# First stage of a two-layer fp32 trunk: modulation weights in row tiles, six convolution chunks in flight, a written order on the engines, later constants on the SP queue

## The chip, the cores and the metric

The kernel runs on one core of a Trainium2 chip. The metric is the device time of one execution in microseconds (us). A core has five engines that run beside each other: TensorE (PE; its weight loads are listed apart as PEld), VectorE (DVE), ScalarE (ACT), GpSimd (POOL) and SyncE (SP). Each takes its instructions in a fixed order, and semaphores hold one back until what it reads has been written. Data come from memory (HBM) by DMA transfers, which an engine's queue issues and 16 DMA engines carry out.

## What is computed

Two layers over 256 latent and 256 context tokens with 1024 features, all in fp32. Each layer modulates its input by a vector worked out from the condition, multiplies it by one wide matrix, and feeds three branches (attention, a depthwise convolution of width 31, pooling), which gates mix; then comes a feed-forward part. The change concerns the beginning of the first layer:

```python
def ada_mod(cond, w, b, n):
    m = jax.nn.silu(cond) @ w[:, :n * D_MODEL] + b[:n * D_MODEL]
    return m.reshape(m.shape[:-1] + (n, D_MODEL))
def modulate(h, shift, scale):
    return h * (1.0 + scale) + shift
...
ml = ada_mod(c, w_ada[l], b_ada[l], N_MOD)[:, None]
mc = ada_mod(c_ctx, w_ada[l], b_ada[l], 2 if last else N_MOD)
hl = modulate(x, ml[..., 0, :], ml[..., 1, :])
hc = modulate(ctx, mc[0], mc[1])
zl = hl @ w_in[l] + b_in[l]
...
# the convolution branch takes 2048 columns of z
a, gt = jnp.split(u, 2, axis=-1)
h = depthwise_conv(a * jax.nn.sigmoid(gt), dw_w, dw_b)
```

So nothing of `w_in` can be multiplied before shift and scale are known, and these need 2048 columns of `w_ada`: 8 MB.

## The kernel before

**Layout.** Activations lie transposed: features on the 128 partitions (eight blocks k of 128), 512 columns of tokens (latent 256, context 256). Each fp32 product is made as three products of fp32r numbers, hi by hi, lo by hi and hi by lo (`mm3`, L326 to L332), where hi is a rounded copy that ACT makes (L228 for weights, L530 for the modulated input) and lo the remainder that DVE subtracts (L229, L339).

**Weights.** They are streamed tile by tile in a written list, `ORDER` (L101). `load_to` (L199 to L212) issues transfers on the SP queue a few places ahead (`LA` = 6) into six raw buffers of 512 KB (`NRAW`); `split_to` (L216 to L230) makes hi and lo in five buffer pairs (`NW`); `take` (L232) hands out the next tile. `x` in the list is a 256 KB tile of the input.

**First stage** (L499 to L546). The modulation is made in four quarters q; each gives shift and scale for two blocks k. `ad0(q, kk)` multiplies the condition (32 columns `sc`) with a 512 KB tile of `w_ada`, four tiles for a quarter, 16 products each (L507). `ad0_end(q)` closes a quarter: DVE copies the row out of PSUM (L514), PE transposes it (L516), DVE adds the bias (L521) and 1 (L525), ACT makes the hi part of the two modulated blocks (L530, four activations), DVE h and its lo part (L531, L339). A convolution chunk is a 512 KB tile of `w_in` with 128 of its columns for all eight k: 24 products (3 by 8) into one PSUM bank. Four such chunks, conv 0 to 3, are started in this stage, each quarter adding the six products of its two k to each of the four banks, with the `ad0` tiles of the next quarter between them.

**Then** chunks conv 4 to 15 run whole (24 products). Chunks come in pairs: ACT takes the sigmoid `sg` of one (L604, its table is loaded first), DVE makes `gl` (L606), and for each two pairs it runs the depthwise taps `H` (L574 first, then L582), which have low priority. Behind conv 15 come the `kv` tiles, the queries, the gates, the pooling. Some 512 KB tiles of `w_ada` (`ada`, L277, eight products) for later modulations lie between the chunks.

**Order.** The Tile framework lays out each engine's order from the program's order and priorities. The constants `ct`, `ID`, `vt[0]`, `ic`, `gr`, `rt`, `vt[1]`, `cb` and the bias rows `bq` are loaded from ACT's queue. `cb` is 1 MB, the condition spread over the partitions, on which ACT then works a Silu (L906).

## Time and profile before

| what | value |
|---|---|
| time, median of 3 runs | 1467.37 us (1467.19 to 1468.29) |
| the profiled execution's own time | 1468.65 us |
| its span, from the first to the last instruction | 1466.8 us |
| PE busy / DVE busy / ACT busy | 1398.2 / 1097.1 / 697.5 us |
| mean granted TensorE clock | 0.986 |
| memory read | 209.83 MB, 144 GB/s over the span |

A row of the timeline reads: start in us, duration in us, engine, line, operation, output<-inputs, tile, count of instructions joined in the row, and in brackets the idle time of the engine before it with what released it. A row of the windows reads: stretch and its length in us, then busy time and count of instructions of each engine in it, the granted TensorE clock (1.00 is full speed, 0.50 half), the mean busy share of the DMA engines and the GB/s that they moved. In the page, a row of digits has one for each fortieth of the span: the busy share in tenths.

### The profile page before, as it was taken

The page shows a single profiled execution, that of the slowest core. Times are in us where ns is not written, and L with a number is a line of the kernel's source. Part 1 is how long each engine was busy: PE and PEld are TensorE (multiplying, and loading weights), DVE is VectorE, ACT ScalarE, POOL GpSimd, SP SyncE. Part 2 cuts the span into 40 slices and gives each one's busy share as a digit, 9 for nine tenths or more (in the row PEclk, how much of TensorE's full clock was granted, in tenths as well). Part 3 has the DMA queues.
Part 4 walks back from the last instruction along what each step waited for, and adds up shares of the span by engine and source line. Part 5 has one row for each costly group of instructions (what it writes and reads, how often), then busy time and mean ns, then how long its engine had stood idle before and what let it go on. Part 6 is the DMA issues. An engine that isn't in the chain of part 4 may idle for free.

```text
span 1466.8 us, 21501 instructions
## 1 busy us (share of the span) xinstructions
PE 1398.2 (95%) x8308; PEld 1207.3 (82%) x8308; DVE 1097.1 (75%) x1998; ACT 697.5 (48%) x1159; POOL 60.2 (4%) x61
## 2 busy tenths in 40 slices
PE   5999999999999998999999999989889989899997
...
DMA  9733332223233411534442677444423345355550
GB/s 368 266 121 131 108 108 94 79 73 121 81 122 130 154 69 58 172 139 162 158 141 93 237 246 251 138 137 139 142 87 130 122 159 181 124 184 187 174 172 29
DMA packets 62246, 212.28 MB, mean 145 GB/s; under 512 B 7104, under 2 KB 8256, under 8 KB 62016
## 3 DMA queue, kind: packets, MB, share of 16 engines
...
q8 instruction: 65, 1.06, 0.3%
...
HBM read 209.83 MB, written 1.05 MB: 144 GB/s over the span
## 4 chain that ended last, share of the span: by engine, by line
PE 64%; issue 15%; DVE 11%; ACT 3%; POOL 1%; DMA 1%; POOLq 0%; DVEq 0%; ACTq 0%
PE mm L330 19%; PE mm L331 19%; PE mm L332 19%; DVE H L582 5%; DVE lo L229 3%; PE ax L362 2%; PE ax L792 1%; PE ax L395 1%; ACT nat L419 1%; PE ad L277 1%; ACT hi L228 1%; DMA rawt<-in_wst 1%; PE ax L434 1%; POOL rotb L663 0%; PE ax L330 0%
## 5 line engine op out<-in xcount | busy, mean ns | idle before, releaser
L228 ACT ACTIVATE hi<-raw 128x1024 fp32r<-128x1024 f32 (+2 forms) x296 | 305.1, 1035 | 495.0 <-PE mm L331 398.8
L229 DVE TENSOR_TENSOR lo<-raw,hi 128x1024 fp32r<-128x1024 f32 (+2 forms) x296 | 353.5, 1197 | 140.0 <-ACT hi L228 134.7
L331 PE MATMUL mm<-hl,hi 128*128 128x256 f32 (+1 forms) x1112 | 353.1, 319 | 2.5 <-DVE hl L471 2.4
L330 PE MATMUL mm<-hh,hi 128*128 128x256 f32 (+1 forms) x1112 | 348.3, 320 | 6.3 <-ACT sg L604 3.2
L332 PE MATMUL mm<-hh,lo 128*128 128x256 f32 (+1 forms) x1112 | 351.6, 318 | 1.9 <-DVE lo L229 1.9
L582 DVE SCALAR_TENSOR_TENSOR H<-gl,vt,H 128x502 f32<-128x502 f32 (+29 forms) x480 | 265.4, 606 | 0.1
L331 PEld LDWEIGHTS mm<-hl,hi 128*128 128x128 f32 x1112 | 214.7, 193 | 18.5 <-DVE hl L471 3.8
L330 PEld LDWEIGHTS mm<-hh,hi 128*128 128x128 f32 x1112 | 211.4, 193 | 22.3 <-ACT sg L604 3.6
L332 PEld LDWEIGHTS mm<-hh,lo 128*128 128x128 f32 x1112 | 214.5, 193 | 16.1 <-DVE lo L229 2.5
L330 PE MATMUL mm<-hi,hi 128*128 128x512 f32 x480 | 192.5, 403 | 0.9 <-ACT hi L530 0.6
L332 PE MATMUL mm<-hi,lo 128*128 128x512 f32 x384 | 151.5, 394 | 0.0
L331 PE MATMUL mm<-llo,hi 128*128 128x512 f32 x384 | 151.2, 394 | 0.0
L330 PE MATMUL mm<-ah,hi 128*128 128x256 f32 (+1 forms) x374 | 123.1, 329 | 0.0
L332 PE MATMUL mm<-ah,lo 128*128 128x256 f32 (+1 forms) x374 | 122.8, 328 | 0.0
L331 PE MATMUL mm<-al,hi 128*128 128x256 f32 (+1 forms) x374 | 122.3, 327 | 0.0
L299 DVE CUSTOM_DVE_ANT_0 prod<-rawt,cb,vt 128x1024 f32<-128x1024 f32 x80 | 102.5, 1281 | 17.5 <-DMA rawt<-in_wst 16.6
L330 PEld LDWEIGHTS mm<-hi,hi 128*128 128x128 f32 x480 | 91.4, 191 | 27.1 <-issue 5.7
L332 PEld LDWEIGHTS mm<-hi,lo 128*128 128x128 f32 x384 | 72.5, 189 | 15.8 <-issue 0.4
L331 PEld LDWEIGHTS mm<-llo,hi 128*128 128x128 f32 x384 | 72.7, 189 | 15.2 <-issue 0.4
L331 PEld LDWEIGHTS mm<-al,hi 128*128 128x128 f32 x374 | 71.0, 190 | 6.0
L330 PEld LDWEIGHTS mm<-ah,hi 128*128 128x128 f32 x374 | 71.0, 190 | 6.0
L332 PEld LDWEIGHTS mm<-ah,lo 128*128 128x128 f32 x374 | 71.0, 190 | 6.0
(178 smaller groups left out, 2017.7 us busy)
## 6 DMA issues: line engine op xcount, KB each, us to landing
raw<-in_wst SPq DMA_DIRECT2D x312, 512.0 KB, 3.5
rawt<-in_wst SPq DMA_DIRECT2D x56, 512.0 KB, 4.1
...
x<-in_xT SPq DMA_DIRECT2D x8, 256.0 KB, 7.1
raw<-in_wst SPq DMA_DIRECT2D x8, 256.0 KB, 2.6
x<-in_xT ACTq DMA_DIRECT2D x8, 256.0 KB, 2.7
bq<-in_brow ACTq DMA_DIRECT2D x6, 256.0 KB, 4.0
...
```

The source lines that it names most:

```text
L228: A.activation(hi[:, :w], r[:, :w], AF.Copy)
L229: V.tensor_tensor(lo[:, :w], r[:, :w], hi[:, :w].bitcast(F32), op=ALU.subtract)
L277: PE.matmul(ps[32 * j:32 * j + 32, :], sc[:, k, :], w[:, j * 256:(j + 1) * 256], start=(k == 0), stop=(k == KT - 1),)
L299: tc.keep_in_program_order(V.tensor_tensor_reduce(prod, w, cb[:, s], 1.0, col(l, "b_ada", m * 8 + c), ALU.mult, ALU.add, mods[l, m][:, c, ...
L330: PE.matmul(ps, lh, rh, start=(first and i == 0), stop=False)
L331: PE.matmul(ps, lh, rl, start=False, stop=False)
L332: PE.matmul(ps, ll, rh, start=False, stop=(last and i == n - 1))
L362: PE.matmul(ps, x[:, a:b], y[:, c:d], start=(i == 0), stop=(i == n - 1))
L395: PE.transpose(a[:, tt * 256 + c2 * P:tt * 256 + (c2 + 1) * P], pair[c2][:, o:o + P], ID)
L419: A.activation(n[:, half(tt)], n[:, half(tt)], AF.Identity, scale=rs[:, tt:tt + 1], bias=nm[:, tt:tt + 1],)
L434: PE.transpose(a[:, c2 * 256 + tt * P:c2 * 256 + (tt + 1) * P], self.nat[i, s][:, o:o + P], ID)
L582: V.scalar_tensor_tensor(h[:, :, a:b], g[:, :, a + d:b + d], col(l, "dw_w", k * 8 + j), h[:, :, a:b], op0=ALU.mult, op1=ALU.add,)
```

## The change

- **Order.** `pin` keeps the instructions of PE, ACT and DVE in the first stage in program order while `strict` is set; the stage is written out as a list of calls. `load` chains the transfers on the SP queue in program order.
- **Six chunks.** conv 4 and conv 5 also start in the first stage, in banks of the `aux` pool; conv 5's hi and lo parts lie in four small `w` tiles, split half by half (there are five buffer pairs for hi and lo).
- **Row tiles.** The first `w_ada` tiles are 32 of 256 KB, 128 rows each, in place of 16 of 512 KB; the host lays them out so. `take` looks 14 places ahead (`LA0`) in this stage.
- **List.** All eight tiles of the first quarter come ahead of any `x`; conv 0 to 5 lie between the tiles of quarters 1 and 2, and quarter 3 is last.
- **Identity products.** 16 products of the identity with itself, into a bank that nobody reads, stand on PE between the first transpose and the first chunk.
- **Constants.** `gr`, `rt`, `vt[1]`, `ic`, `cb` and all `bq` move from the ACT queue to the SP queue, in program order behind weights.

On SP, at the program's start, the order was this (`raw` are weight tiles, `x` input tiles):

```order
L212 DMA raw_95<-in_wst 128x1024
L212 DMA raw_97<-in_wst 128x1024
L205 DMA x_99<-in_xT 128x512
L205 DMA x_101<-in_xT 128x512
L212 DMA raw_103<-in_wst 128x1024
L212 DMA raw_105<-in_wst 128x1024
L212 DMA raw_107<-in_wst 128x1024
L212 DMA raw_113<-in_wst 128x1024
L212 DMA raw_115<-in_wst 128x1024
```

And now it is this, from the first quarter's last tiles on (`ad` are the 256 KB tiles of `w_ada`):

```order
L202 DMA ad_108<-in_wst 128x512
L202 DMA x_110<-in_xT 128x512
L202 DMA x_112<-in_xT 128x512
L202 DMA raw_114<-in_wst 128x1024
L202 DMA raw_116<-in_wst 128x1024
L202 DMA ad_118<-in_wst 128x512
L202 DMA ad_120<-in_wst 128x512
L202 DMA ad_122<-in_wst 128x512
L202 DMA ad_129<-in_wst 128x512
L202 DMA raw_135<-in_wst 128x1024
```

The first quarter's 2 MB no longer have the two `x` tiles between them, and conv 0 (`raw_107` before, `raw_114` now) and conv 1 (`raw_115`, `raw_116`) follow directly on `x`.

On ACT, the program's beginning was this; row by row it issues constants and then works:

```order
L178 DMA ct<-in_cT 128x16
L179 DMA ID<-in_ident 128x128
L181 DMA vt_80<-in_vec 128x524
L183 DMA ic<-in_icnt 128x64
L265 ACT_TABLE_LOAD
L265 ACTIVATE sc<-ct 128x8x2
L617 DMA gr<-in_grow 128x512
L627 DMA vt_81<-in_vec 128x524
L628 DMA cb<-in_crow 128x2048
L637 DMA bq_1059<-in_brow 128x512
L906 ACTIVATE cb<-cb 128x2048
L228 ACTIVATE hi_109<-raw_107 128x1024
```

And now:

```order
L186 DMA ct<-in_cT 128x16
L187 DMA ID<-in_ident 128x128
L189 DMA vt_80<-in_vec 128x524
L297 ACT_TABLE_LOAD
L297 ACTIVATE sc<-ct 128x8x2
L564 ACTIVATE hi_195<-x_110,mod_0_91,one_p 128x256 x2
L564 ACTIVATE hi_203<-x_112,mod_0_91,one_p 128x256 x2
L260 ACTIVATE hi_217<-raw_114 128x1024
L260 ACTIVATE hi_224<-raw_116 128x1024
```

Five transfers and the Silu of `cb` have gone from here. On SP they now stand between weight tiles for chunks behind the first stage (`rt` is the rotation table, `raw_556` and `raw_880` weight tiles):

```order
L202 DMA raw_556<-in_wst 128x1024
L202 DMA gr<-in_grow 128x512
L202 DMA rt_765<-in_rope 128x512
L202 DMA vt_81<-in_vec 128x524
L202 DMA ic<-in_icnt 128x64
L202 DMA cb<-in_crow 128x2048
L202 DMA raw_880<-in_wst 128x1024
```

Before, SP had only weight tiles there. The Silu of `cb` now comes behind the sigmoid of conv 9, with a table load ahead of it and one behind.

On PE, between the first and the second round of chunk products, this stood before (`ad_335` and `ad_415` are quarters 2 and 3 of the modulation, `ax` a transposed row, `mm_197`, `mm_247` conv 0 and conv 1 with the blocks of quarter 1):

```order
L516 MATMUL ax_308<-ID,adarow_306 128x128
L507 MATMUL ad_335<-raw_215,sc 32x128 x8
L507 MATMUL ad_335<-raw_217,sc 32x128 x8
L507 MATMUL ad_335<-raw_223,sc 32x128 x8
L507 MATMUL ad_335<-raw_225,sc 32x128 x8
L516 MATMUL ax_388<-ID,adarow_386 128x128
L507 MATMUL ad_415<-raw_227,sc 32x128 x8
L507 MATMUL ad_415<-raw_229,sc 32x128
L330 MATMUL mm_197<-hi_313,hi_109 128x512
L330 MATMUL mm_247<-hi_313,hi_117 128x512
```

And this stands there now (`ax_305` is quarter 1's transposed row, `mm_316` conv 3 with quarter 0, `ad_345` quarter 2, `mm_221` conv 0 with quarter 1):

```order
L548 MATMUL ax_305<-ID,adarow_303 128x128
L362 MATMUL mm_316<-hi_195,hi_312 128x512
L363 MATMUL mm_316<-xlo_197,hi_312 128x512
L364 MATMUL mm_316<-hi_195,lo_313 128x512
L362 MATMUL mm_316<-hi_203,hi_312 128x512
L363 MATMUL mm_316<-xlo_205,hi_312 128x512
L364 MATMUL mm_316<-hi_203,lo_313 128x512
L540 MATMUL ad_345<-ad_215,sc 32x128 x4
L540 MATMUL ad_345<-ad_222,sc 32x128 x4
L540 MATMUL ad_345<-ad_235,sc 32x128 x4
L540 MATMUL ad_345<-ad_242,sc 32x128 x4
L362 MATMUL mm_221<-hi_317,hi_217 128x512
```

Before, all of quarter 2 and the beginning of quarter 3 (and the transfers they wait for) stood ahead of the second round; now half of quarter 2 does, and a chunk's products stand behind the transpose.

On PE at the program's start there is now (`ax_178` is the bank of the identity products, `mm_221` conv 0):

```order
L548 MATMUL ax_173<-ID,adarow_171 128x128
L582 MATMUL ax_178<-ID 128x128 x16
L362 MATMUL mm_221<-hi_195,hi_217 128x512
L363 MATMUL mm_221<-xlo_197,hi_217 128x512
L364 MATMUL mm_221<-hi_195,lo_218 128x512
```

Nothing stood between this transpose and the next `ad0` tiles before. Behind the first stage the orders of the engines agree but for the constants above and a few exchanges of neighbours; on DVE five lo parts (conv 6 to 10) stand ahead of the first tap, where four did (conv 4 to 7).

The diff, without the definitions of constants and the change to the host's layout:

```diff
+    first = [[("ad0", 0, q, k) for k in range(KT)] for q in range(4)]
+    xs = [[("x", 0, 2 * q), ("x", 0, 2 * q + 1)] for q in range(4)]
     o = weight_order(0)
-    conv = [x for x in o if x[0] == "conv"][:4]
-    res = first[0] + [conv[0]] + first[1][:1] + [conv[1]] + first[1][1:4] + [conv[2]] + first[1][4:5] + [conv[3]] + first[1][5:]
-    return res + first[2] + first[3] + [x for x in o if x not in conv] + weight_order(1)
+    conv = [x for x in o if x[0] == "conv"][:NCP]
+    res = first[0] + xs[0] + conv[:2] + first[1][:4] + conv[2:3] + first[1][4:] + conv[3:4] + xs[1]
+    res += first[2][:4] + conv[4:5] + first[2][4:] + conv[5:6] + xs[2] + xs[3] + first[3]
+    return res + [x for x in o if x not in conv] + weight_order(1)
...
+    def pin(ins):
+        return tc.keep_in_program_order(ins) if strict else ins
...
+    def load(dst, src, behind=True):
+        i = SP.dma_start(dst, src).ins
+        if behind and loads:
+            tc.add_manual_dep(
+                i, loads[-1].name, mybir.DependencyInfo(mybir.DependencyClass.NoSync, mybir.DependencyReason.DATA),
+                reason="order of loads",
+            )
+        loads.append(i)
...
+            if it[0] == "ad0":
+                raw[it] = S(name="ad0")
+                load(raw[it], wst[o:o + P * w].rearrange("(p c) -> p c", p=P))
...
+            if strict and it == ("conv", 0, 2, 1):
+                split[it] = tuple(tuple(S(F32R, "w") for _ in range(2)) for _ in range(2))
+                for x, (hi, lo) in enumerate(zip(*split[it])):
+                    rx = r[:, x * 512:(x + 1) * 512]
+                    pin(A.activation(hi, rx, AF.Copy))
+                    pin(V.tensor_tensor(lo, rx, hi.bitcast(F32), op=ALU.subtract))
+                continue
...
-            load_to(i + LA)
-            split_to(ahead[i])
+            load_to(i + (LA0 if strict else LA))
+            split_to(i if strict else ahead[i])
...
-    for kk in range(4):
-        ad0(0, kk)
+    ad0(0, range(8))
     ad0_end(0)
-    for q in range(4):
-        for i in range(4):
-            it = ("conv", 0, i // 2, i % 2)
-            if q == 0:
-                convpre[it] = take(it), mmb()
-            mm_by_k([convpre[it]], hT, (2 * q, 2 * q + 1), NTOK)
-            if q < 3:
-                ad0(q + 1, i)
-        if q < 3:
-            ad0_end(q + 1)
+    warm = aux()
+    for _ in range(NWARM):
+        pin(PE.matmul(warm[:, :P], ID, ID, start=True, stop=True))
+    scaled(0)
+    conv_take(0, 1)
+    conv_mm(0, 0)
+    ad0(1, range(4))
+    conv_mm(0, 1)
+    conv_take(2)
+    conv_mm(0, 2)
+    ad0(1, range(4, 8))
+    ad0_end(1)
+    conv_take(3)
+    scaled(1)
+    conv_mm(0, 3)
+    ad0(2, range(4))
+    conv_mm(1, 0, 1, 2, 3)
+    conv_take(4)
+    conv_mm(0, 4)
+    ad0(2, range(4, 8))
+    conv_mm(1, 4)
+    ad0_end(2)
+    conv_take(5)
+    scaled(2)
+    conv_mm(0, 5)
+    conv_mm(1, 5)
+    conv_mm(2, 0, 1, 2, 3)
+    ad0(3, range(8))
+    conv_mm(2, 4)
+    ad0_end(3)
+    scaled(3)
+    conv_mm(2, 5)
+    conv_mm(3, *range(NCP))
+    strict.clear()
...
-                A.dma_start(gr, grow[l:l + 1, :].to_broadcast([P, 512]).rearrange("p (a d) -> p a d", a=4))
+                load(gr, grow[l:l + 1, :].to_broadcast([P, 512]).rearrange("p (a d) -> p a d", a=4))
...
-                    A.dma_start(cb, crow.to_broadcast([P, 2 * D]).rearrange("p (s d) -> p s d", s=2))
+                    load(vt[1], vec[1])
+                    load(ic, icnt.to_broadcast([P, 64]).rearrange("p (g e t) -> p g e t", g=4, e=2))
+                    load(cb, crow.to_broadcast([P, 2 * D]).rearrange("p (s d) -> p s d", s=2))
...
-            A.dma_start(bq, brow[l:l + 1, boff:boff + 512].to_broadcast([P, 512]))
+            load(bq, brow[l:l + 1, boff:boff + 512].to_broadcast([P, 512]))
```

In the diff, `scaled(q)` holds L530, L531 and L339 of `ad0_end` as it was, `conv_take` takes chunks and gives them banks, and `conv_mm(q, ...)` adds quarter q's products to the chunks named.

More of the change, by code (lines that the diff above doesn't have):

```diff
@@ L35 @@
 LA = 6
+LA0 = 14
+NCP = 6
+NWARM = 16
 LS = 3
@@ L101, in full_order @@
 def full_order():
-    first = [
-        [("ad0", 0, q, 0), ("ad0", 0, q, 1), ("x", 0, 2 * q), ("x", 0, 2 * q + 1), ("ad0", 0, q, 2), ("ad0", 0, q, 3)]
-        for q in range(4)
-    ]
+    first = [[("ad0", 0, q, k) for k in range(KT)] for q in range(4)]
+    xs = [[("x", 0, 2 * q), ("x", 0, 2 * q + 1)] for q in range(4)]
     o = weight_order(0)
-    conv = [x for x in o if x[0] == "conv"][:4]
-    res = first[0] + [conv[0]] + first[1][:1] + [conv[1]] + first[1][1:4] + [conv[2]] + first[1][4:5] + [conv[3]] + first[1][5:]
-    return res + first[2] + first[3] + [x for x in o if x not in conv] + weight_order(1)
+    conv = [x for x in o if x[0] == "conv"][:NCP]
+    res = first[0] + xs[0] + conv[:2] + first[1][:4] + conv[2:3] + first[1][4:] + conv[3:4] + xs[1]
+    res += first[2][:4] + conv[4:5] + first[2][4:] + conv[5:6] + xs[2] + xs[3] + first[3]
+    return res + [x for x in o if x not in conv] + weight_order(1)
 ORDER = full_order()
@@ L118, in width @@
         return 0
-    if it[0] == "plw":
+    if it[0] in ("plw", "ad0"):
         return 512
@@ L204, in load_to @@
                 xr.append(S(name="x"))
-                SP.dma_start(xr[-1], xT[it[2]])
+                load(xr[-1], xT[it[2]])
+                nxt["load"] += 1
+                continue
+            if it[0] == "ad0":
+                raw[it] = S(name="ad0")
+                load(raw[it], wst[o:o + P * w].rearrange("(p c) -> p c", p=P))
                 nxt["load"] += 1
@@ L211, in load_to @@
                 t = wp.tile([P, CH], F32, tag="raw", name=f"raw{nxt['load']}", bufs=NRAW)
[L212 removed]
+            load(t[:, :w], wst[o:o + P * w].rearrange("(p c) -> p c", p=P), bool(strict) or it[0] == "adt")
             raw[it] = t
@@ L329, in mm3 @@
         for i, ((lh, ll), (rh, rl)) in enumerate(pairs):
-            PE.matmul(ps, lh, rh, start=(first and i == 0), stop=False)
-            PE.matmul(ps, lh, rl, start=False, stop=False)
-            PE.matmul(ps, ll, rh, start=False, stop=(last and i == n - 1))
+            pin(PE.matmul(ps, lh, rh, start=(first and i == 0), stop=False))
+            pin(PE.matmul(ps, lh, rl, start=False, stop=False))
+            pin(PE.matmul(ps, ll, rh, start=False, stop=(last and i == n - 1)))
     def part(hl, a, b):
+        if isinstance(hl[0], tuple):
+            return tuple(x[a // 512][:, a % 512:a % 512 + b - a] for x in hl)
         return hl[0][:, a:b], hl[1][:, a:b]
@@ L497, in trunk, with ad0 @@
     ad0_ps = {}
-    def ad0(q, kk):
-        w = take(("ad0", 0, q, kk))
-        if kk == 0:
-            ad0_ps[q] = pad.tile([P, 256], F32, tag="ad", name=uid("ad"))
-        for k2 in range(2):
-            for j in range(4):
-                o = k2 * 512 + j * P
-                PE.matmul(
-                    ad0_ps[q][32 * j:32 * j + 32, :P], sc[:, 2 * kk + k2, :], w[:, o:o + P],
-                    start=(kk + k2 == 0), stop=(kk + k2 == 4),
-                )
+    def ad0(q, ks):
+        for k in ks:
+            w = take(("ad0", 0, q, k))
+            if k == 0:
+                ad0_ps[q] = pad.tile([P, 256], F32, tag="ad", name=uid("ad"))
+            for j in range(4):
+                pin(PE.matmul(
+                    ad0_ps[q][32 * j:32 * j + 32, :P], sc[:, k, :], w[:, j * P:(j + 1) * P], start=(k == 0), stop=(k == KT - 1),
+                ))
     def ad0_end(q):
         row = sm(256, "adarow", bufs=1)
-        V.tensor_copy(row[:, :P], ad0_ps[q][:, :P])
+        pin(V.tensor_copy(row[:, :P], ad0_ps[q][:, :P]))
         pt = aux()
-        PE.transpose(pt[:, :P], row[:, :P], ID)
+        pin(PE.transpose(pt[:, :P], row[:, :P], ID))
         hk = slice(2 * q, 2 * q + 2)
@@ L526, in ad0_end, with scaled @@
+    def scaled(q):
         for k in (2 * q, 2 * q + 1):
-            hi, h32 = S(F32R, name="hi"), S(name="h32")
+            hi, h32, lo = S(F32R, name="hi"), S(name="h32"), S(F32R, name="xlo")
             for s in range(2):
                 sh, sl = mods[0, 0][:, k, s:s + 1], one_p[:, k, s:s + 1]
-                A.activation(hi[:, half(s)], xr[k][:, half(s)], AF.Identity, scale=sl, bias=sh)
-                V.tensor_scalar(h32[:, half(s)], xr[k][:, half(s)], sl, sh, op0=ALU.mult, op1=ALU.add)
```

33 lines of the change are left out of this document (21 added, 12 removed).

## The prediction

> **What bounds the kernel now.** First the page: the whole span, then its digits.
>
> ```profile
> span 1466.8 us, 21501 instructions
> PE 1398.2 (95%) x8308; PEld 1207.3 (82%) x8308; DVE 1097.1 (75%) x1998; ACT 697.5 (48%) x1159; POOL 60.2 (4%) x61
> PE   5999999999999998999999999989889989899997
> DMA  9733332223233411534442677444423345355550
> ```
>
> PE is busy 95% of the span, so the time follows what PE does; its one weak digit is the first (5), where the DMA engines show 9. So I cut the beginning into stretches with the windows.
>
> ```profile
> 0.00:12.00 12.00, 1.93 (x32) 1.38 (x32) 1.06 (x12) 1.50 (x2) 0.45 (x8) 1.00 0.79 290
> 12.00:22.00 10.00, 4.25 (x58) 2.50 (x59) 2.96 (x7) 4.74 (x5) 0.00 (x0) 1.00 1.03 409
> 22.00:36.00 14.00, 12.13 (x133) 7.54 (x128) 5.94 (x12) 5.37 (x9) 0.00 (x0) 0.98 1.03 405
> 36.00:44.00 8.00, 7.61 (x39) 5.43 (x36) 6.00 (x16) 2.07 (x4) 0.00 (x0) 0.60 1.03 404
> 44.00:62.40 18.40, 17.40 (x128) 11.85 (x126) 7.01 (x13) 6.79 (x9) 0.00 (x0) 1.00 0.63 229
> 66.00:123.00 57.00, 57.00 (x258) 46.61 (x257) 57.00 (x78) 13.51 (x15) 4.52 (x4) 1.00 0.36 126
> 123.00:143.00 20.00, 20.00 (x101) 15.41 (x100) 5.38 (x6) 5.03 (x6) 0.00 (x0) 1.00 0.40 137
> 182.00:187.00 5.00, 2.43 (x9) 2.04 (x10) 4.99 (x12) 3.45 (x18) 3.27 (x4) 0.88 0.19 44
> ```
>
> Up to 22 us PE works 6.2 us of 22, up to 44 the DMA engines are full at some 405 GB/s, and in 36 to 44 the granted clock is 0.60. From 66 to 123 PE and DVE are both full; in 123 to 143 DVE is free for 14.6 of 20 us; in 182 to 187 PE waits beside a full DVE. The timeline of PE shows what the first stage waits for.
>
> ```profile
> 12.81 1.08 PE L507 MATMUL ad<-raw,sc 128*32 128x128 f32 x16 [4.63 <-DMA raw<-in_wst]
> 15.91 1.08 PE L507 MATMUL ad<-raw,sc 128*32 128x128 f32 x16 [2.02 <-DMA raw<-in_wst]
> ...
> 22.46 1.22 PE L330 MATMUL mm<-hi,hi 128*128 128x512 f32 x2
> ...
> 24.79 0.63 PE L332 MATMUL mm<-hi,lo 128*128 128x512 f32 x1
> ...
> 31.46 0.27 PE L516 MATMUL ax<-ID,adarow 128*128 128x128 f32 x1
> 31.66 1.08 PE L507 MATMUL ad<-raw,sc 128*32 128x128 f32 x32
> 33.96 0.65 PE L507 MATMUL ad<-raw,sc 128*32 128x128 f32 x16 [1.22 <-DMA raw<-in_wst]
> ...
> 38.38 1.65 PE L330 MATMUL mm<-hi,hi 128*128 128x512 f32 x3
> ...
> 42.63 0.40 PE L332 MATMUL mm<-hi,lo 128*128 128x512 f32 x1
> ...
> 62.78 0.50 PE L330 MATMUL mm<-hi,hi 128*128 128x512 f32 x1 [0.35 <-ACT sg L604]
> ...
> 129.84 0.39 PE L330 MATMUL mm<-hi,hi 128*128 128x512 f32 x1
> ```
>
> The first chunk product starts at 22.46, conv 4 at 62.78, and the `kv` products at 129.84. Between the rounds of quarters 0 and 1 PE has no chunk product from 31.46 to 38.38: it waits for quarter 2's tiles, which stand ahead. That stretch also brings the slow clock: the ten products from 38.38 to 42.63 take 4.25 us.
>
> **The price of a chunk.** Twelve chunks (conv 4 to 15) and two `ada` tiles lie between 62.78 and 129.84. What an inserted tile costs is read here:
>
> ```profile
> 106.25 0.39 PE L332 MATMUL mm<-hi,lo 128*128 128x512 f32 x1
> 106.57 0.64 PE L277 MATMUL ad<-raw,sc 128*32 128x256 f32 x8
> 107.14 0.50 PE L330 MATMUL mm<-hi,hi 128*128 128x512 f32 x1
> ```
>
> From 106.25 to 107.14 are 0.89 us; less one product's 0.23, the insert costs 0.66. So a chunk is (67.06 - 1.32) / 12 = 5.478 us, a product 0.228 us.
>
> **Part 1: when the data come.** By 12 us 3.48 MB had moved (12 x 290), then 0.405 MB a us. How far work is behind that:
>
> ```profile
> 24.08 1.06 ACT L228 ACTIVATE hi<-raw 128x1024 fp32r<-128x1024 f32 x1 [0.89 <-DMA raw<-in_wst]
> 15.76 1.91 ACT L906 ACTIVATE cb<-cb 128x2048 f32<-128x2048 f32 x1 [9.57 <-DMA cb<-in_crow]
> ```
>
> conv 2's tile ends 22 units of 256 KB on SP, with 2.2 MB from ACT's queue (1 MB of it `cb`) beside them: 7.97 MB, moved by 23.0; ACT starts at 24.08. I take 1.15 us of lag. After the change ACT's queue brings 0.33 MB. By the new list the first quarter's eight tiles (2.4 MB) land at 10.6 (the last one's products now run from 15.91), the two `x` at 11.9, conv 0 at 13.2, conv 1 at 14.5, quarter 1's halves at 17.0 and 20.9 with conv 2 at 18.3 between, conv 3 at 22.2, quarter 2's first half at 26.1, conv 4 at 27.4, its second half at 30.0, conv 5 at 31.3, quarter 3 at 39. The gain here is the 1.9 MB of constants that no longer compete, and a better order.
>
> **Part 2: from the last `ad0` product to a chunk.** The fourth quarter shows the steps undisturbed:
>
> ```profile
> 53.70 0.29 DVE L514 COPY adarow<-ad 128x128 f32<-128x128 f32 x1 [7.13 <-PE ad L507]
> 54.82 2.08 ACT L530 ACTIVATE hi<-x,mod,one_p 128x256 fp32r<-128x256 f32 x4 [9.50 <-DVE one_p L525]
> 55.96 1.19 PE L330 MATMUL mm<-hi,hi 128*128 128x512 f32 x4 [0.58 <-ACT hi L530]
> 75.06 1.21 DVE L229 TENSOR_TENSOR lo<-raw,hi 128x1024 fp32r<-128x1024 f32 x1
> ```
>
> From copy to chunk are 2.26 us. In the first quarter conv 0 is also split behind the modulated blocks: copy at about 11, ACT's four activations (2.08) from 12.2, conv 0's hi (1.06) from 14.3, so its first product could run at 15.4. The 16 identity products lie in this wait, from 11.9 on. At the 0.20 us from 31.46 to 31.66 they take 3.2, all at half clock 6.4. The first chunk products were slow up to about 25 (0.63 at 24.79), 2.5 us behind their start at 22.46; so I take the first eight at double: 4.8, and conv 0 starts at 16.7.
>
> **Part 3: PE's chain.** conv 0 ends at 18.1 (six products, 1.4), quarter 1's first half at 19.0, conv 1 at 20.4, conv 2 (landed 18.3, split 2.2) at 21.8, quarter 1's second half (landed 20.9) at 22.8, conv 3 at 25.9 (its lo stands behind `one_p` on DVE: copy to `one_p` 1.1, lo 1.2, the products left 0.8), quarter 2's first half, landed 26.1, at 26.9. That is the last place where a transfer is near to ending a wait. With 3.2 for the identity products this point is 26.5, with 6.4 it is 28.5. From there the sum is PE's own work: 120 chunk products (conv 0 to 3 in quarters 1 and 2, conv 4 and 5 in quarters 0 to 2, all six in quarter 3) x 0.228 = 27.4; three half quarters of modulation 3.05 (a half is 32 records, 1.08 at 31.66); two transposes 0.55; waits for conv 5's lo behind `one_p` and for quarter 3's `xlo`, 0.8 and 0.85, the latter filled by part of two `ada` tiles, whose rest is 0.35. Together 33.0: conv 6 starts at 59.9.
>
> Before, conv 4 started at 62.78. So the lead is 2.88, plus two chunks already done (10.96), less one `ada` tile that now comes later (0.66): **13.2 us**, with `kv` at 116.6. The same by losses:
>
> ```profile
> L507 PE MATMUL ad<-raw,sc 128*32 128x128 f32 x256 | 14.2, 345 | 17.3 <-DMA raw<-in_wst 11.0 <-ACT sc L265 6.2
> ```
>
> What PE must do before `kv` is 16 chunks (87.7), eight half quarters (8.6), five `ada` tiles (3.3), transposes (1): 100.6 of 129.84, so 29.2 is lost. Idle is 19.4 of it (62.4 less the 43.3 busy in the windows, and 0.35 at 62.78); the rest is slow products (this group alone 14.2 for 8.6). After, 24 chunk products, five half quarters and two transposes are such work up to 26.9, 11.4: 15.5 lost, and some 0.7 later. 29.2 - 16.2 is 13.0, as near as the parts are rounded.
>
> **Part 4: what follows.** A lead must get past DVE, which is full up to 123.
>
> ```profile
> 60.75 1.28 ACT L604 ACT_TABLE_LOAD   x1
> 66.64 1.00 DVE L574 TENSOR_SCALAR H<-gl,vt 128x512 f32<-128x512 f32 x2
> 136.57 1.23 DVE L229 TENSOR_TENSOR lo<-raw,hi 128x1024 fp32r<-128x1024 f32 x1 [3.78 <-ACT hi L228]
> ```
>
> conv 0 and 1 end at about 56.5 now; the table load, sigmoid, `gl` and lo parts follow, and the first tap comes at about 64.8: only 1.8 earlier, with three more lo parts behind it (3 x 1.14). So DVE is 5.2 ahead, PE 13.2. The missing 8.0 come out of DVE's 14.6 idle in 123 to 143, where it waits for hi parts (136.57) whose buffers PE frees, and those come earlier with PE. In between, lo parts stand tiles ahead of their use; by the order and these durations the tightest margin is that of `gl` behind conv 12 and 13, where both come at about 105.7. I take no loss.
>
> The Silu of `cb` leaves the start of ACT's queue and costs 1.91 + 2 x 1.28 = 4.5 behind conv 9; ACT is busy 13.5 of 57 there, which hides it (without that cover, a sigmoid 4.5 late). `gr`, `rt`, `vt[1]`, `ic`, `cb` now load from SP, 1.9 MB between weight tiles at 126 GB/s of a possible 405: nothing. Each `bq` waits on SP until the sums that read the last one are done, with weight tiles queued behind it; PE has about seven tiles of work in hand there (six raw buffers and a split one), 7 x 5.48 = 38 us: nothing; if that cover were gone, see E.
>
> **Sum.** The profiled execution took 1468.65, span 1466.8 and 1.85 around it, 1.28 over the median. 1468.65 - 13.2 = 1455.45; by the median, 1467.37 - 13.2 = **1454.2**.
>
> **The skill against the rows.** The ten products from 38.38 show 0.43 us each, twice the 0.228. The Trainium skill, page "TensorE: Matmul & The Clock Gate", section "What's actually happening", says that the array's default is half clock and that a free-running window of some 3.4 us of activity releases it; the rows agree in the ratio, and by it the identity products would bring conv 0 to full clock at no price, or a part of it, as the window falls. Of transfers of 256 KB instead of 512 KB the row is this:
>
> ```profile
> raw<-in_wst SPq DMA_DIRECT2D x312, 512.0 KB, 3.5
> x<-in_xT SPq DMA_DIRECT2D x8, 256.0 KB, 7.1
> bq<-in_brow ACTq DMA_DIRECT2D x6, 256.0 KB, 4.0
> ```
>
> The `x` tiles lie in stretches that moved 405 GB/s all the same. The Trainium skill, "DMA: Bandwidth & Descriptors", section "Bandwidth", says to batch transfers to 1 MiB or more for 75% of the peak, which speaks against this change. Its "Anatomy of one DMA" fits 2.0 us and bytes by 436 GB/s; an estimate from that page, 16 more transfers over eight in flight, is 4 us, half of it before 26.9, and the sum would be 1456.2.
>
> **Rivals.**
> - B, the half clock comes again, since PE's work between 18 and 26 has holes: one stretch costs 4.25 - 10 x 0.228 = 2.0 us, two 4.0: **1458.2**. For it: 36 to 44 at 0.60, behind a hole. Against it is this row, 68% busy and at full clock:
>
> ```profile
> 210.00:215.00 5.00, 3.41 (x18) 2.62 (x17) 5.00 (x10) 2.80 (x12) 3.27 (x3) 1.00 0.28 105
> ```
>
> - C, small tiles move slower: at the first stretch's 290 GB/s instead of 405, quarter 2's first half (8.7 MB) lands at 31.2, 5 later: **1459.2**. Against it: the `x` tiles.
> - D, DVE becomes the bound and only its 5.2 are kept: **1462.2**. For it: 57 of 57 us in 66 to 123. Against it: the 14.6 behind.
> - F, all of it is given back in the wait at 182 to 187, where PE stands idle beside a full DVE, so that the wait grows by the lead: **1467.4**. For it: 2.43 of 5; against it, DVE gets its inputs earlier too.
> - E, slower: a waiting `bq` holds SP's queue. If its wait outlasts PE's 38 us in hand, each of the four that wait for an earlier reader costs a landing and a split, 3.5 + 1.06 + 1.2 = 5.8, 23.2 in all: **1477.4**. Against it: a reader is done within a few us of its last tile's products.
>
> **Chances.** A measurement of this kernel tells some 0.2% (2.9 us) from no change. Forecast 0.62 (1454.2), B 0.12, C 0.09, D 0.07, F 0.05, E 0.05. Faster is A, the forecast, with B, C and D: 0.90; same F, 0.05; slower E, 0.05. The forecast's own range is 1450.5 (identity products at 3.2, 0.4; the two waits vanish, 1.65; the queues fill as much earlier) to 1456.9 (identity products at 6.4, 1.6, and half a DVE margin lost, 1.1); the range asked for reaches over B and C to 1460.5.
>
> **What would show it.** In the profile after: first chunk product near 16.7, quarter 2's first half near 26, conv 6 near 59.9, `kv` near 116.6; granted clock 1.00 from 17 on; first tap near 64.8; DVE's idle in the 20 us behind `kv` shrunk by about 8; no SP wait for `bq`'s reader that a chunk waits for. `kv` later than 121 makes the first stage wrong; `kv` in time and the end not 13 earlier makes part 4 wrong.

## The result, and the profile after

| | time, median | gain |
|---|---|---|
| before | 1467.97 us (1467.19 to 1469.28, 6 runs) | |
| after | 1458.82 us (1458.48 to 1460.46, 6 runs) | 9.15 us |
| forecast | 1454.2 us (range 1450.5 to 1460.5) | 13.2 us |

The ratio of the two is 0.9938, with a 95% interval of 0.9925 to 0.9951. The profiled execution took 1459.06 us, its span is 1457.3. The change made the kernel faster, by 4 us less than forecast. The range that was given reaches over the rivals B and C to 1460.5, and 1458.82 lies in it; the forecast's own range ended at 1456.9, and 1458.82 lies 1.9 us above that. Where the 4 us are is the question of what follows.

The page after, the same lines as before:

```profile
span 1457.3 us, 21593 instructions
PE 1397.7 (96%) x8340; PEld 1209.6 (83%) x8340; DVE 1097.2 (75%) x1999; ACT 700.4 (48%) x1162; POOL 62.0 (4%) x61
PE   7999899999999999999999999889799989899997
DMA  9543332323232521444442777344323345355550
```

PE's first digit went from 5 to 7; its busy time is the same to 0.5 us. The DMA engines' first digits went from 9733 to 9543: the constants are read in the third slice now (`gr` lands at 85.6, `cb` at 89.8). The windows of the stretches that the prediction spoke of (stretch and length, busy time of PE, PEld, DVE, ACT, POOL with counts, granted clock, DMA share, GB/s):

```profile
11.18:16.63 5.45, 5.45 (x34) 5.45 (x33) 4.68 (x11) 3.97 (x6) 0.00 (x0) 1.00 1.03 394
16.63:28.34 11.71, 9.92 (x124) 6.65 (x122) 5.74 (x12) 4.20 (x6) 0.00 (x0) 1.00 1.04 391
28.34:62.38 34.04, 33.45 (x238) 25.21 (x234) 11.87 (x26) 10.37 (x16) 0.00 (x0) 1.00 0.61 227
66.00:123.00 57.00, 57.00 (x267) 45.45 (x266) 56.62 (x78) 18.55 (x19) 7.81 (x4) 1.00 0.51 184
123.00:143.00 20.00, 20.00 (x98) 15.88 (x97) 13.75 (x26) 5.78 (x13) 0.00 (x0) 1.00 0.37 124
174.00:182.00 8.00, 7.96 (x26) 6.45 (x27) 5.68 (x10) 2.98 (x10) 1.75 (x2) 0.68 0.35 100
```

From 28.34 on PE is busy and at full clock, where it stood at 0.60 in 36 to 44 before. PE's timeline after, at the places of the chain:

```profile
11.18 5.70 PE L582 MATMUL ax<-ID 128*128 128x128 f32 x32
16.63 0.49 PE L362 MATMUL mm<-hi,hi 128*128 128x512 f32 x1
...
19.22 0.50 PE L362 MATMUL mm<-hi,hi 128*128 128x512 f32 x1
...
20.96 0.40 PE L363 MATMUL mm<-xlo,hi 128*128 128x512 f32 x1
21.66 0.50 PE L364 MATMUL mm<-hi,lo 128*128 128x512 f32 x1 [0.30 <-DVE lo L261]
...
26.20 0.50 PE L364 MATMUL mm<-hi,lo 128*128 128x512 f32 x1 [1.07 <-DVE lo L261]
...
27.00 0.40 PE L364 MATMUL mm<-hi,lo 128*128 128x512 f32 x1
27.33 1.08 PE L540 MATMUL ad<-ad,sc 128*32 128x128 f32 x32
28.34 0.50 PE L362 MATMUL mm<-hi,hi 128*128 128x512 f32 x1
...
39.21 0.50 PE L364 MATMUL ax<-hi,w 128*128 128x512 f32 x1 [0.59 <-DVE w L256]
...
51.78 0.40 PE L364 MATMUL ax<-hi,w 128*128 128x512 f32 x1
52.10 0.62 PE L309 MATMUL ad<-raw,sc 128*32 128x256 f32 x2
52.65 0.49 PE L362 MATMUL mm<-hi,hi 128*128 128x512 f32 x1
53.08 0.64 PE L309 MATMUL ad<-raw,sc 128*32 128x256 f32 x8
53.65 0.50 PE L363 MATMUL mm<-xlo,hi 128*128 128x512 f32 x1
...
62.38 0.50 PE L362 MATMUL mm<-hi,hi 128*128 128x512 f32 x1
...
119.32 0.39 PE L362 MATMUL mm<-hi,hi 128*128 128x512 f32 x1
```

The 16 identity products (32 records) run from 11.18; conv 0 starts at 16.63 (16.7 forecast), the second round at 28.34 (26.9), conv 6 at 62.38 (59.9), `kv` at 119.32 (116.6). Before, `kv` started at 129.84: the lead there is 10.5 us, not 13.2. So 2.7 of the missing 4 us are lost up to `kv` (2.5 of them up to conv 6), and the rest behind it.

In the runs that follow, the place to read is this lead at `kv`. It comes from one profile each, and two profiles of the changed kernel gave 10.5 and 10.8. The times of whole executions scatter more: those of the kernel before from 1465.64 to 1472.16 in 20 runs.

### The profile page after: what moved, and what is told of

Same layout as the page of the kernel before. It is cut to its first block, busy times and chain, and to the rows that moved or that the text cites. A ratio compares the mean times of both kernels' runs of the same rounds, so it can differ in the third digit from the quotient of the medians.

```text
span 1457.3 us, 21593 instructions
## 1 busy us (share of the span) xinstructions
PE 1397.7 (96%) x8340; PEld 1209.6 (83%) x8340; DVE 1097.2 (75%) x1999; ACT 700.4 (48%) x1162; POOL 62.0 (4%) x61
## 5 line engine op out<-in xcount | busy, mean ns | idle before, releaser
L362 PEld LDWEIGHTS mm<-hh,hi 128*128 128x128 f32 x1112 | 211.4, 193 | 22.2 <-ACT sg L671 3.6
L362 PE MATMUL mm<-hi,hi 128*128 128x512 f32 x464 | 186.1, 401 | 0.0
L364 PE MATMUL mm<-hi,lo 128*128 128x512 f32 x368 | 144.5, 393 | 1.4 <-DVE lo L261 1.4
L363 PE MATMUL mm<-xlo,hi 128*128 128x512 f32 x368 | 144.0, 391 | 0.0
L362 PEld LDWEIGHTS mm<-hi,hi 128*128 128x128 f32 x464 | 87.8, 189 | 25.0 <-issue 5.7
L364 PEld LDWEIGHTS mm<-hi,lo 128*128 128x128 f32 x368 | 69.1, 188 | 16.8 <-DVE lo L261 2.2
L363 PEld LDWEIGHTS mm<-xlo,hi 128*128 128x128 f32 x368 | 69.2, 188 | 13.9 <-issue 0.4
```

The costliest lines, as they stand in the source:

```text
L362: pin(PE.matmul(ps, lh, rh, start=(first and i == 0), stop=False))
L363: pin(PE.matmul(ps, lh, rl, start=False, stop=False))
L364: pin(PE.matmul(ps, ll, rh, start=False, stop=(last and i == n - 1)))
```

## The experiments

**Theories.** T: up to 28 us the landing of transfers sets PE's pace, bytes and their order count, and the identity products lie in a wait; from there PE's own work and the holes in it. O: the written order and the six chunks make the gain, the constants' bytes are hidden. C: the clock is the point, and the identity products keep it up.

| kernel | median us (runs) | ratio to before, 95% interval | conv 0 | second round | `kv` | lead |
|---|---|---|---|---|---|---|
| after, again | 1458.46 (5) | 0.9935 [0.9924, 0.9947] | 16.39 | 28.02 | 119.01 | 10.8 |
| no identity products | 1459.47 (6) | 0.9935 [0.9920, 0.9950] | 14.40 | 28.15 | 119.14 | 10.7 |
| 40 identity products | 1464.67 (12) | 0.9968 [0.9956, 0.9980] | 21.40 | 32.50 | 123.52 | 6.3 |
| constants on ACT's queue | 1464.71 (9) | 0.9974 [0.9963, 0.9984] | 21.60 | 34.70 | 125.67 | 4.2 |
| before, constants on SP | 1464.81 (12) | 0.9971 [0.9962, 0.9980] | 17.04 | 33.70 | 124.68 | 5.2 |
| four chunks | 1464.43 (6) | 0.9967 [0.9954, 0.9979] | 16.68 | 28.07 | 123.45 | 6.4 |
| not pinned | 1462.89 (5) | 0.9965 [0.9953, 0.9977] | 22.28 | 34.15 | 122.10 | 7.5 |
| tiles of 512 KB | 1456.92 (4) | 0.9922 [0.9908, 0.9936] | 14.21 | 27.12 | 118.11 | 11.7 |
| 512 KB, conv 5 split early | 1458.07 (5) | 0.9929 [0.9918, 0.9941] | 14.09 | 27.25 | 117.39 | 12.4 |
| the same, no identity | 1459.19 (6) | 0.9937 [0.9924, 0.9949] | 14.81 | 27.71 | 117.85 | 12.0 |

The columns behind the ratio are starts on PE in the profile, and the lead of `kv` over the 129.84 of the kernel before.

### No identity products

```diff
-NWARM = 16
+NWARM = 0
-    warm = aux()
```

> The changed kernel without its 16 identity products. Theory T (up to 28 us the landing of transfers sets PE's pace, and the identity products lie in a wait): conv 0 starts at about 15.1 instead of 16.63, its six products at half clock take 2.6 us and end near 17.7, quarter 1's first half lands at 17.95 and conv 2 at 19.26 as before, so the second round starts within 0.5 us of 28.34 and the time is within 1 us of 1458.8. Rival C (clock: without them the half clock stays or comes back in the holes up to 27 us): one or two stretches of 2.0 us each, 1460.8 to 1462.8.

Measured: 1459.47, lead 10.7. PE's timeline of this run, then one row of ACT's, the split of conv 2:

```profile
14.40 0.80 PE L362 MATMUL mm<-hi,hi 128*128 128x512 f32 x1 [3.51 <-ACT hi L260]
14.99 0.63 PE L363 MATMUL mm<-xlo,hi 128*128 128x512 f32 x1
...
17.77 1.94 PE L540 MATMUL ad<-ad,sc 128*32 128x128 f32 x32
19.64 0.50 PE L362 MATMUL mm<-hi,hi 128*128 128x512 f32 x1
...
22.60 1.08 PE L540 MATMUL ad<-ad,sc 128*32 128x128 f32 x32
...
28.15 0.50 PE L362 MATMUL mm<-hi,hi 128*128 128x512 f32 x1
```

```profile
17.58 1.06 ACT L260 ACTIVATE hi<-raw 128x1024 fp32r<-128x1024 f32 x1 [2.29 <-DMA raw<-in_wst]
```

conv 0 starts 2.2 us earlier, at half clock (products of 0.63), and quarter 1's first half runs at half clock too (1.94 for 32 records where 1.08 is usual). At 19.64 the clock is full, and the second round starts 0.2 us earlier than with the products.

The number of theory T came, but this profile doesn't show its mechanism. From the start of conv 0 to the end of that half quarter PE takes 5.24 us (14.40 to 19.64) where the changed kernel takes 2.59 (16.63 to 19.22). So the slow products cost 2.65 us (a wait of 0.15 among them), where C has 2.0 for a stretch at half clock. Two things pay for it. conv 0 starts 2.23 us earlier. And conv 2's tile, which ACT splits from 17.58 here and from 19.29 in the changed kernel, came earlier: PE has no wait for its lo, which in the changed kernel costs 0.58 us (0.70 from 20.96 to 21.66 where 0.23 is usual, and 0.11 behind it). 2.65 - 2.23 - 0.58 is -0.16, and the second round starts 0.19 earlier. PE's own work sets the pace here, from 15.77 to 24.10, not a landing. So the half clock costs at least what C has for it, and still the time is no longer: identity products ahead of conv 0 take about as long as the full clock saves. What brings the clock to full is any work of PE.

### Forty identity products

```diff
-NWARM = 16
+NWARM = 40
```

> The changed kernel with 40 identity products instead of 16. The trace has 0.117 us a record and 0.23 us a product once the clock is full, so 24 more take 5.6 us and conv 0 starts at about 22.2 instead of 16.63. Theory T: of these 5.6 some 2 us are hidden by the waits up to 26.2 (0.3 and 1.07 in the timeline, and 0.7 at half landing), the second round starts near 31.9 and the time is 3 to 4 us longer, 1462. If PE's place before 28 us were of no account (all of it hidden behind transfers), it would be 1458.8; if nothing is hidden, 1464.4.

Measured: 1464.67, lead 6.3, so 4.2 us less. The products end and conv 0 starts at 21.40, 4.8 later than with 16; the second round starts at 32.50, 4.2 later. About 0.6 us were hidden, less than the 2 expected. It is the wait for conv 2's lo, which is gone in this profile: PE has none between 21.40 and 28.42. So PE's chain up to 28 us has that much slack and no more, and theory T is half right for this stage: PE's own work sets the pace nearly as much as the landings do. Together with the run before it: removing 2.2 us at conv 0 gains 0.2, since the half clock takes the rest, and adding 4.8 costs 4.2.

### The constants on ACT's queue again

```diff
-                load(gr, grow[l:l + 1, :]...
+                A.dma_start(gr, grow[l:l + 1, :]...
```

and so for `rt`, `vt[1]`, `ic`, `cb` and `bq`.

> The changed kernel with the constants gr, rt, vt[1], ic, cb and bq issued from ACT's queue again, whose order puts five of them and the Silu of cb at the program's start. Theory T: 1.87 MB more compete before the weights of the first stage; at 390 GB/s all landings behind come 4.8 us later, the second round starts near 33 instead of 28.34, and the time is 4 to 5 us longer: 1463.3. Rival O (the order on the engines and the six chunks make the gain, the transfers have slack): less than 1 us longer, 1459.5.

Measured: 1464.71, lead 4.2, so 6.3 us less. PE's timeline and then ACT's:

```profile
15.62 0.65 PE L540 MATMUL ad<-ad,sc 128*32 128x128 f32 x8 [3.35 <-DMA ad<-in_wst]
...
16.95 4.89 PE L582 MATMUL ax<-ID 128*128 128x128 f32 x32
```

```profile
15.13 1.91 ACT L974 ACTIVATE cb<-cb 128x2048 f32<-128x2048 f32 x1 [9.77 <-DMA cb<-in_crow]
17.60 2.07 ACT L564 ACTIVATE hi<-x,mod,one_p 128x256 fp32r<-128x256 f32 x4 [0.56 <-DVE one_p L557]
```

The first quarter's last products end at 16.27 (15.62 and 0.65) instead of 10.49, and everything behind is late by about as much: the second round starts at 34.70, 6.4 later. That is theory T in what it says of bytes, and even more than the 4.8 us that they would take at 390 GB/s. The Silu of `cb`, for which ACT waits 9.77 us, isn't the cause: it ends at 17.04, and ACT still waits 0.56 us for `one_p` behind it.

### The kernel before with the constants on SP

```diff
+    def load(dst, src, behind=True):
...
-                A.dma_start(gr, grow[l:l + 1, :]...
+                load(gr, grow[l:l + 1, :]...
```

and so for the other constants; weight tiles take `load(..., False)`, and nothing else is changed.

> The kernel before with one part of the change alone: gr, rt, vt[1], ic, cb and bq issued from SP behind weight tiles; all else as before. Theory T (in the first stage the time goes by the landing of transfers, so the bytes ahead of them count): 1.9 MB less ahead at 400 GB/s, all landings 4 to 5 us earlier, the second round starts near 34 instead of 38.38, and 5 us are gained, 1463; 2 us more if the half clock behind the hole does not come. Rival O (the gain is the written order and the six chunks): under 1.5 us, 1467.

Measured: 1464.81, lead 5.2, so this part alone brings half of the lead. PE's timeline and the windows of this run:

```profile
33.70 1.65 PE L340 MATMUL mm<-hi,hi 128*128 128x512 f32 x3
```

```profile
28.00:32.00 4.00, 1.84 (x33) 1.08 (x33) 0.29 (x1) 0.79 (x2) 0.00 (x0) 0.75 1.03 399
32.00:38.00 6.00, 6.00 (x32) 4.41 (x32) 5.19 (x15) 2.08 (x4) 0.00 (x0) 0.60 1.03 408
```

The hole ahead of the second round is still there (1.84 of 4 us busy), with the half clock behind it; the whole stage has moved by 4.7 to 5.4 us.

### Four chunks in place of six

```diff
-NCP = 6
+NCP = 4
```

and the calls for conv 4 and 5 taken out of the first stage.

> The changed kernel with four chunks in the first stage in place of six (conv 4 and 5 come behind it, whole). Theory T: the second round starts at 28.3 as before; with no chunk 4 and 5 to fill them, the chains from the last modulation product to the next round (2.3 us each, quarters 2 and 3) are idle, less two ada tiles of 0.66 in the second, so the lead at kv is 1.5 to 3 us smaller than 10.5 and the time 1460.5 to 1462; a half clock behind such a hole costs 2.0 more. Rival S6 (the two chunks done ahead, 10.96 us, are the gain): 5 us or more longer, 1464 and up.

Measured: 1464.43, lead 6.4, so 4.1 us less. PE's timeline, then the windows:

```profile
35.23 0.33 PE L548 MATMUL ax<-ID,adarow 128*128 128x128 f32 x1 [0.41 <-DVE adarow L546]
37.14 0.50 PE L362 MATMUL mm<-hi,hi 128*128 128x512 f32 x1 [1.58 <-ACT hi L564]
...
49.27 0.49 PE L362 MATMUL mm<-hi,hi 128*128 128x512 f32 x1 [0.63 <-ACT hi L564]
```

```profile
33.50:37.00 3.50, 1.65 (x35) 0.95 (x33) 1.40 (x6) 1.00 (x3) 0.00 (x0) 1.00 1.05 392
37.00:42.00 5.00, 4.63 (x12) 3.44 (x13) 2.23 (x5) 2.13 (x4) 0.00 (x0) 0.66 1.03 409
```

The second round starts as before, at 28.07. Behind it, PE waits for the modulated blocks of quarter 2 (0.41 and 1.58) and of quarter 3, and behind the first hole comes the half clock (0.66 in 37 to 42), which the prediction had priced at 2.0 a stretch. The upper end of theory T with one such stretch is 5.0, the lower 3.5: 4.1 lies between. The loss isn't the 10.96 us of two chunks, as S6 has it; these only fill 4.1 us that were empty or slow. By whole times S6 seems nearer: the gain over the kernel before falls from 9.15 to 4.53 us, and 1464.43 is within its "1464 and up". But in this profile the lead falls from 6.5 us at 930 to 3.0 at the end, far behind the stage that was edited (see below).

### Not pinned

```diff
-        return tc.keep_in_program_order(ins) if strict else ins
+        return ins
```

> The changed kernel without the pin on PE, ACT and DVE: the scheduler orders the first stage itself, the loads stay in their chain. It puts all of quarter 2's tiles ahead of the second round, which then waits for their landing (31.3) and starts at about 31.5 instead of 28.34; conv 4's first six products (1.4) and half a quarter (1.1) are done by then. Theory T: 0.7 to 1.5 us longer, 1460. Rival P (the pinned order is the main part): 4 us or more longer.

Measured: 1462.89, lead 7.5, so 3.0 us less; expected were 0.7 to 1.5. PE's timeline and then ACT's:

```profile
18.23 1.08 PE L540 MATMUL ad<-ad,sc 128*32 128x128 f32 x32
20.88 0.43 PE L540 MATMUL ad<-ad,sc 128*32 128x128 f32 x8 [1.56 <-DMA ad<-in_wst]
21.54 0.43 PE L540 MATMUL ad<-ad,sc 128*32 128x128 f32 x8 [0.24 <-DMA ad<-in_wst]
22.28 0.96 PE L362 MATMUL mm<-hi,hi 128*128 128x512 f32 x3 [0.31 <-ACT hi L564]
```

```profile
20.19 1.06 ACT L260 ACTIVATE hi<-raw 128x1024 fp32r<-128x1024 f32 x1 [3.15 <-DMA raw<-in_wst]
21.15 2.06 ACT L564 ACTIVATE hi<-x,mod,one_p 128x256 fp32r<-128x256 f32 x4
```

I had looked at PE's order ahead of the second round; what decides is ACT's order ahead of the first. Six tiles of quarter 1 stand ahead of conv 0 on PE, and PE waits 1.8 us for two of them, but the wait that ends last is for the hi parts of quarter 0's modulated blocks (0.31, ACT L564). On ACT the splits of conv 0, 1 and 2 stand ahead of these blocks now, and the third waits for its landing. So the blocks are made from 21.15 on, though DVE's `one_p` was ready at 12.97; with the pin it is from 11.82. conv 0 starts 5.7 us later than with the pin, and a part of that is filled. Not all of the 3.0 us need be the order's: in this profile the transfers land later from the start, and the first transpose comes at 12.09 instead of 10.91.

### Tiles of 512 KB

```diff
+                if it[3] % 2 == 0:
+                    r = 4 * it[2] + it[3] // 2 in (0, 1, 6, 7, 10, 11, 12, 13)
+                    t = wp.tile([P, CH], F32, tag="rawt" if r else "raw", ...)
+                    load(t, wst[o:o + 2 * P * w].rearrange("(p c) -> p c", p=P))
+                    raw[it], raw["ad0", 0, it[2], it[3] + 1] = t[:, :512], t[:, 512:]
```

> The changed kernel with the first modulation weights in pairs, 16 tiles of 512 KB (4 KB a partition) in place of 32 of 256 KB, in the same order; eight buffers of the weight pools hold them. Theory T (bytes and their order count, not the size of a tile): within 1 us of 1458.8. Rival S (small tiles move slower, 391 GB/s instead of 405 from 16 to 40 us): landings at 27 us come 0.5 us earlier, up to 1 us faster, 1458.0. Rival L (a row tile lets PE begin on half a pair): the first quarter's last products start 0.5 us later, 1459.3.

Measured: 1456.92, lead 11.7, 1.2 (0.9 against the other profile) more than the changed kernel. The windows of 16 to 28 us, of the changed kernel and then of this one:

```profile
16.00:28.00 12.00, 10.21 (x121) 7.14 (x124) 6.12 (x13) 4.20 (x6) 0.00 (x0) 1.00 1.03 390
```

```profile
16.00:28.00 12.00, 9.94 (x123) 6.55 (x122) 6.38 (x13) 5.08 (x7) 0.00 (x0) 1.00 1.03 407
```

The queues move 407 GB/s with 512 KB and 390 with 256 KB. Rival S, then, with about the size that it gave. The edit also takes buffers of the weight tiles: the queue waits up to 6.4 us for one behind this and moves 238 GB/s in 28 to 34, but PE is busy in all of these 6 us.

### Conv 5 split early, and without identity products

```diff
-    ad0_end(2)
     conv_take(5)
+    ad0_end(2)
     scaled(2)
```

> The changed kernel with 512 KB pairs of modulation tiles and with conv 5's split ahead of the end of quarter 2, where DVE is idle, instead of behind it. The wait of 0.6 us for conv 5's lo (0.8 with the restart) goes. Against the pairs alone (1456.9, lead at kv 11.7): lead at kv 12.4, time 1456.2. Rival: the copy of the row comes later behind the split and gives it back, 1456.9.

Measured: 1458.07, lead 12.4: the wait at 39.21 is gone and the lead at `kv` is 0.7 larger, as expected; the whole time doesn't show it.

> The changed kernel with 512 KB pairs of modulation tiles, conv 5's split ahead of the end of quarter 2, and no identity products. Theory T: the identity products lie in slack here too; conv 0 starts at about 14 at half clock and ends near 17, the landings of quarter 1 and conv 2 set the pace: lead at kv 12.4 as with them (within 0.3), time 1457, 2 us under the changed kernel. Rival C (clock): 2 us less lead, 1459.

Measured: 1459.19, lead 12.0, 0.4 less than with the products, where theory T had at most 0.3. In PE's starts, conv 0 runs at half clock from 14.81 and quarter 1's first half starts at 18.19 instead of 16.59, its second half at 22.16 instead of 21.70. But the first transpose, ahead of all this, came at 10.82 in this profile and at 10.24 in the other. These 0.58 us are more than the 0.4, so what the full clock is worth with 512 KB tiles isn't shown.

> The changed kernel once more, unaltered, beside the next one on the same chip. Lead at kv over the kernel before 10.5 us (within 0.5, by where a DMA engine falls behind); time 1458.8, and the same 9 us of gain.

Measured: 1458.46 and a lead of 10.8. So the three kernels with 512 KB tiles lead by 11.7 to 12.4 us at `kv` where three profiles with 256 KB (these two, and the one without identity products) have 10.5 to 10.8; by that 512 KB is the better size, with one profile of each kernel but this one. In whole times, the intervals of the ratios overlap (0.9922 [0.9908, 0.9936] the best of them, 0.9935 [0.9924, 0.9947] the changed kernel again), and it isn't shown.

## Why the prediction was right, and where it was off

**Direction and mechanism** held. Constants out of the way, the row of holes closed, no half clock from 16.63 to 143. Undoing one part at a time costs 6.3 (constants), 4.1 (chunks 4 and 5), 3.0 (the pinned order) and -0.2 us (identity products) of a lead of 10.5; going back to 512 KB gains 1.2. These don't add up to 10.5: with the constants alone the kernel before gains 5.2, so the parts share holes. The pinned order's 3.0 may hold up to 1.2 of late landings, as said.

That the measured 1458.82 lies nearer to B's 1458.2 and C's 1459.2 than to the forecast's 1454.2 is chance: the half clock of B did not come in this stage, and C's 5 us of later landings were 0.9. The range holds the measured time only because it was drawn over these two.

**Up to the second round: steps of PE that were sized too small, and a landing.** The sum had the second round at 26.9, and it came at 28.34, 1.44 later. Step by step: conv 0 is 0.07 early; the wait for conv 2's lo, for which the sum has nothing, costs 0.58; quarter 1's second half and conv 3 behind it take 4.55 (22.78 to 27.33) instead of 4.1; the other steps take some 0.1 more each, 0.5 together, since the first product behind a change of kind is followed after 0.34 us instead of 0.228. Only the 0.58 are a landing. With conv 2 landed 1.7 us earlier, in the profile without identity products, that wait is gone.

**Part 1, the landings.** I took 1.15 us from the bytes to the landing. ACT's timeline shows conv 2 and conv 3, forecast to land at 18.3 and 22.2:

```profile
19.29 1.06 ACT L260 ACTIVATE hi<-raw 128x1024 fp32r<-128x1024 f32 x1 [3.49 <-DMA raw<-in_wst]
23.29 1.06 ACT L260 ACTIVATE hi<-raw 128x1024 fp32r<-128x1024 f32 x1 [2.94 <-DMA raw<-in_wst]
```

The trace has 16 landings for each transfer. Of quarter 2's first half (forecast 26.1) these are the first and the last, and of an earlier transfer:

```
run                        quarter 1, first half    quarter 2, first half
                           first  last  spread      first  last  spread
after                      15.62 17.95   2.33       24.92 27.29   2.37
after, again               15.74 16.79   1.05       25.05 26.97   1.92
no identity products       15.72 16.28   0.56       25.03 27.07   2.04
tiles of 512 KB            14.97 16.93   1.96       24.01 25.80   1.79
```

By the bytes the forecast was right: 26.1 less 1.15 is 24.95, and the first part landed at 24.92. But a spread of 0.4 to 1.1 us becomes one of 1.8 to 2.4 at some transfer whose first part lands between 15 and 22 us, and stays so while the queue is full; with 512 KB tiles, where the queue runs empty behind 32 us, the spread is 0.5 at 37.6. At that step it is one part of the 16 that falls behind, and the last but one keeps its place. The whole transfer then comes 1.2 us later than I took. Such a step, of 0.8 to 1.6 us, is in ten of the twelve profiles, in that of the kernel before too (0.71 to 1.54, at 27.44, behind the row at 24.08 from which I took the lag). With four chunks it is 0.4, and in the kernel that isn't pinned the spread is 1.4 to 2.7 from 5 us on. What it is the traces don't show.

The landing that the prediction called the last one near to ending a wait, of quarter 2's first half, is 1.2 us late (27.29) and ends none even so: its products start 0.33 us behind the product ahead (27.00 to 27.33). With 512 KB tiles, where the half lands 0.3 us before, it is 0.32 (25.79 to 26.11).

**Part 2** held: conv 0 at 16.7 was forecast and came at 16.63, with luck, since two errors cancel: the products took 5.45 us from 11.18, not 4.8 from 11.9. That 0.4 us was to be had from shorter products no run shows; without any of them it was 0.2, and the half clock came instead.

**Part 3, PE's own 33.0 us** were 34.04. The two `ada` tiles and the `xlo` wait were forecast at 1.2: the three gaps around them are 0.87, 1.00 and, at 61.50 to 62.38, 0.88, less a product each 2.06. The transposes cost 0.06, not 0.55. The wait for conv 5's lo was 0.76 (0.8). What remains is the first product behind each insert, whose next one starts 0.34 us later (28.34, 39.21) instead of 0.228, seven times. Of the 2.5 us by which conv 6 is late, 1.4 come up to the second round (0.6 of them conv 2's landing) and 1.0 here.

**Part 4 held where it mattered, with a wrong step.** DVE's timeline after:

```profile
67.60 1.00 DVE L641 TENSOR_SCALAR H<-gl,vt 128x512 f32<-128x512 f32 x2
...
123.32 1.34 DVE L649 SCALAR_TENSOR_TENSOR H<-gl,vt,H 128x482 f32<-128x482 f32 x2
```

The first tap comes at 67.60, 1.0 later than before and 2.8 later than forecast, where conv 6 is 2.5 late. The last tap of this first run ends at 124.66, not 5.2 earlier but 1.6 later than before. The step that failed is that three lo parts fewer lie between the two taps: DVE makes ten there, as before, since those of later tiles move up. Even so PE is busy all of 66 to 123: the lo parts stood far enough ahead. The idle time of DVE from 123 to 143 went from 14.6 to 6.2, 8.4 less, and 8.0 were forecast to be taken from there. So D, the rival of a binding DVE, falls by its slack and not by its lead. E and F fell. PE is busy all of 123 to 143, where `bq` is first used. The wait that F would lengthen is 4.07 us before (up to 184.57) and 4.08 now (up to 174.04). Of 10.5 us lead at 180 us 9.5 are left at 187 in one profile, 10.7 of 10.8 in the other: behind that wait the clock is at half, for 6.8 us in the one (the row of 174 to 182, at 0.68) and for 3.4 in the other and in the kernel before. B did not come. Without conv 4 and 5 the half clock comes once, but in 37 to 42 and not where B had it, in 18 to 26. C, the smaller tiles, was right in direction, but its 5 us were 0.9 by the landings.

**Behind `kv`.** The two profiles end with 9.6 and 10.5 us of lead; the medians with 9.15 and 9.75 (1468.21 less 1458.46). Between 940 and 1000 us the lead changes by 1 to 3 us in most profiles, up or down, and the granted clock differs there from kernel to kernel. The same window of the kernel before and of the one with four chunks:

```profile
960.00:975.00 15.00, 13.01 (x104) 12.60 (x104) 13.88 (x30) 7.71 (x12) 2.30 (x2) 0.98 0.33 114
```

```profile
960.00:975.00 15.00, 11.05 (x69) 10.65 (x68) 15.00 (x27) 3.54 (x4) 3.32 (x4) 0.77 0.38 124
```

In the kernel with four chunks, the lead falls from 6.5 us at 930 to 4.0 at 1000; in the profile without identity products it grew from 11.0 to 13.0. What sets it isn't settled; the forecast had no term for it.

**The size of the tiles, and the clock.** The Trainium skill, "DMA: Bandwidth & Descriptors", section "Bandwidth", spoke against the smaller tiles, and the trace agrees: 390 GB/s against 407, and 0.9 us by the first landing at 8.7 MB (24.92 against 24.01). The estimate of 2 us from the fit in "Anatomy of one DMA" was twice that; that fit and the section's table are for DMAs that GpSimd issues, and these are issued by SyncE. The same skill's "TensorE: Matmul & The Clock Gate", section "What's actually happening", agrees with the runs in that activity of PE releases the half clock (full from 19.64 without the identity products) and in the length of its window, some 3.4 us: most stretches at half clock in these traces last 3.4 us or twice that. But the prediction, beside its sum, took from it that identity products come at no price or a part of it. They run at half clock themselves until 15.2, overrun the wait that they stand in, and cost about what they save.
